# Decoder layer on one core: recurrence products moved from GpSimd to VectorE, two phases merged, and several smaller moves

## Chip, cores and metric

The kernel runs on one core of one Trainium2 chip. The time is that of one execution on the device in microseconds, from the runs of the same program. All times below that are placed inside an execution count from the first instruction of the profiled execution.

## What is computed

One layer of a decoder for 512 positions of width 1024, all in 32-bit floats. The part of the reference that matters here:

```python
h = rms_norm(x, g_pre_mix)
z = h @ w_in                                   # 512 x 1024 by 1024 x 9776 or so, cut in pieces
u, v, q, kv, nsa_g, xr, rg, mg = split(z)
y_a = gmlp_mixer(gelu(u), gelu(v), ...)        # LayerNorm of v, 128-position chunks, lower-triangular w_s
y_b = nsa_mixer(q, kv, nsa_g, ...)             # attention; its compress MLP: gelu((blocks + pe) @ w1) @ w2
y_c = rglru_mixer(xr, rg, ...)
merged = sum_k sigmoid(mg_k) * (y_k @ w_br_k)
x = x + rms_norm(merged @ w_o, g_post_mix)
f_gate, f_up = split(rms_norm(x, g_pre_ffn) @ w_ffn_in)
x = x + rms_norm((silu(f_gate) * f_up) @ w_ffn_out, g_post_ffn)

def rglru_mixer(xr, gate, ...):
    xc = conv4(xr) + conv_b                    # causal, per channel, along the positions
    r = sigmoid(xc @ w_a + b_a)                # 16 diagonal blocks of 64 x 64
    i = sigmoid(xc @ w_x + b_x)
    a = exp(-8 * r * softplus(-lam))
    b = sqrt(1 - a * a) * (i * xc)
    h[t] = a[t] * h[t - 1] + b[t]              # linear scan along the positions
    return h * gelu(gate)
```

## The kernel before

**Products.** Each product of 32-bit matrices is made of three TensorE products of rounded halves: high by high, high by low, low by high. `split` (L112 on) makes the halves: ScalarE copies the rounded high half (L114), VectorE subtracts it from the source for the low half (L119). The weights pass in tiles of 128x1024 (512 KB) through the sync engine's queue: `unit()` hands out the next weight tile, and `wload` fetches and splits two more ahead of it, with two buffers for the raw tile and three each for its halves. A tile of output is 24 products of 512 columns (8 blocks of the inner dimension by 3).

**Order.** The work is written as Python generators that `yield` at places where other work may be put between. `run(main, side, rate)` walks through the main generators and steps the side one `rate` times per yield. A main generator that yields a number n goes on a list: it has done its product, and its remaining steps come after n more yields of the main generators behind it, so that what it needs next from other engines can be made meanwhile. `seq` makes one side generator of several. The phases around the change are the calls of `run` from L1202 on:

```python
run([v_half(0), v_half(1), cmp_tile(0)], seq(norm(), load_wab()))
run(rnn(0, 0, 4), softplus())
run([gate_tile(), cmp_tile(1), cmp_tile(2)], seq(rec_batch(0), rec_out(0)))
run(rnn(1, 0, 4))
run([cmp_tile(3), gate_part("c", 0), compress(0), gate_part("c", 1)], seq(rec_batch(1), rec_out(1)))
```

**The recurrent branch.** It is cut in two halves of four tiles of 128 channels. `xr_tile` (L410) makes a tile's input product, the convolution on VectorE (L422), the split of the convolved rows (`ch` on ScalarE, `cl` on VectorE), and after `yield 3` the two gate products on TensorE (L430; bank `tr`, output R and TI). `rg_tile` makes the other input product and its gelu (GG). `rec_batch` (L439) then does the recurrence of a half: tanh, root and exponentials on ScalarE, and for each tile of 128x512 a small product on VectorE (L454), one on GpSimd (L455) and the scan on VectorE (L457). `rec_out` (L466) multiplies with the gelu on GpSimd (L473) and splits the result (`ych`, `ycl`) for the branch products.

**Beside it.** `gate_tile` makes the gates of the attention branches (`gsig`, transposed at L601), `cmp_tile` a part of the rows for compress (`xcmp`, copied by ScalarE at L623 and VectorE at L624), `compress` the small MLP of the attention: its first weights come as two 1 MB loads issued on ScalarE's queue (L630, tile `w`), its inputs are made by GpSimd's additions, its products are at L648, its hidden layer (`chid`) from L655 on. `gmlp_prep` (L480) loads the gMLP's triangle and bias (tile `gw`). `down` and its `close` (L1125) end the kernel: the last product, its sum of squares, the root, and the residual sum, by tiles of 128 positions in two halves of 512 columns.

**Buffers and banks.** SBUF tiles stand in pools by tag (slab 3, y 4, m 2, wab 2 buffers of 128x2048), PSUM in banks `mm` (6) and `tr` (2). Inside an engine the instructions run in the order in which they are issued, and across engines they are held by semaphores that the framework sets; the DMA issues of SP, ScalarE and GpSimd stand in those engines' own order.

## Time and profile before

| | |
|---|---|
| runs | 1162.02, 1164.91, 1165.14 us; median 1164.91 |
| profiled execution | 1168.17 us, of which the span of the instructions is 1166.4 us |
| mean granted TensorE clock in it | 0.991 of full speed |
| busy share | TensorE 98%, VectorE 59%, ScalarE 46%, GpSimd 5% |
| chain that ended last | TensorE 87% of the span, VectorE 7%, DMA 3%, ScalarE 2% |

The profiled execution is 3.3 us over the median of the runs. The rows below are of this one execution. In them PE is TensorE, PEld its weight loads, DVE VectorE, ACT ScalarE, POOL GpSimd, SP the sync engine; a name with q behind it (ACTq) is that engine's queue, where DMAs are issued. L12 is line 12 of the kernel before. Tiles bear the program's names.

### The profile page before, as it was taken

The page shows a single profiled execution, that of the slowest core. Times are in us where ns is not written, and L with a number is a line of the kernel's source. Part 1 is how long each engine was busy: PE and PEld are TensorE (multiplying, and loading weights), DVE is VectorE, ACT ScalarE, POOL GpSimd, SP SyncE. Part 2 cuts the span into 40 slices and gives each one's busy share as a digit, 9 for nine tenths or more (in the row PEclk, how much of TensorE's full clock was granted, in tenths as well). Part 3 has the DMA queues.
Part 4 walks back from the last instruction along what each step waited for, and adds up shares of the span by engine and source line. Part 5 has one row for each costly group of instructions (what it writes and reads, how often), then busy time and mean ns, then how long its engine had stood idle before and what let it go on. Part 6 is the DMA issues. An engine that isn't in the chain of part 4 may idle for free.

```text
span 1166.4 us, 14306 instructions
## 1 busy us (share of the span) xinstructions
PE 1140.9 (98%) x5524; PEld 949.6 (81%) x5524; DVE 690.6 (59%) x1266; ACT 532.8 (46%) x936; POOL 55.2 (5%) x55
## 2 busy tenths in 40 slices
PE   9999799999999999999999999999999999999997
PEld 7877578788888887888888788889988888888885
DVE  5974855545476799998898743557333323322324
ACT  6746446222244576877776523344323223232222
POOL 0000702510000000000000000000000000000001
PEclk9999989899999999999999999999999999999999
DMA  8332222522222211112111343332132232232231
GB/s 286 116 108 73 69 76 65 209 92 90 94 87 91 72 55 37 55 41 69 37 55 55 110 145 107 116 119 73 55 103 96 91 106 93 92 125 91 93 106 72
DMA packets 30373, 108.62 MB, mean 93 GB/s; under 512 B 3649, under 2 KB 3793, under 8 KB 29153
## 3 DMA queue, kind: packets, MB, share of 16 engines
q1 hardware_dynamic: 27792, 98.58, 25.7%
q10 hardware_dynamic: 2448, 9.05, 2.1%
q8 instruction: 43, 0.70, 0.2%
q14 instruction: 26, 0.20, 0.1%
q0 software_dynamic: 64, 0.08, 0.0%
HBM read 105.60 MB, written 2.10 MB: 92 GB/s over the span
## 4 chain that ended last, share of the span: by engine, by line
PE 87%; DVE 7%; DMA 3%; ACT 2%; issue 1%; POOL 1%; SPq 0%; DVEq 0%; ACTq 0%; POOLq 0%
PE mm L212 57%; PE mm L1122 10%; PE mm L1022 4%; PE sc L816 3%; PE o L854 3%; PE tr L841 3%; PE mm L732 2%; DVE lo L119 1%; PE tr L648 1%; PE tr L430 1%; DMA wabr<-in_wab 1%; DMA xrow<-in_x 1%; DVE ti L457 1%; PE tr L564 1%; DMA xt<-in_xT 1%
## 5 line engine op out<-in xcount | busy, mean ns | idle before, releaser
L114 ACT ACTIVATE hi<-raw 128x1024 fp32r<-128x1024 f32 (+1 forms) x162 | 170.8, 1054 | 357.6 <-PE mm L212 160.7
L119 DVE TENSOR_TENSOR lo<-raw,hi 128x1024 fp32r<-128x1024 f32 (+1 forms) x162 | 199.6, 1233 | 220.4 <-ACT hi L114 212.6
L212 PE MATMUL mm<-hh,lo 128*128 128x512 f32 x504 | 199.5, 396 | 2.5 <-DVE lo L119 2.5
L212 PE MATMUL mm<-hh,hi 128*128 128x512 f32 x504 | 200.5, 398 | 0.0
L212 PE MATMUL mm<-hl,hi 128*128 128x512 f32 x504 | 198.8, 395 | 0.0
L212 PE MATMUL mm<-fh,hi 128*128 128x512 f32 (+1 forms) x336 | 127.6, 380 | 0.0
L212 PE MATMUL mm<-fh,lo 128*128 128x512 f32 (+1 forms) x336 | 127.3, 379 | 0.0
L212 PE MATMUL mm<-fl,hi 128*128 128x512 f32 (+1 forms) x336 | 127.3, 379 | 0.0
L212 PEld LDWEIGHTS mm<-hh,lo 128*128 128x128 f32 x504 | 95.7, 190 | 22.8 <-DVE lo L119 3.4
L212 PEld LDWEIGHTS mm<-hl,hi 128*128 128x128 f32 x504 | 95.5, 189 | 18.9 <-issue 0.2
L212 PEld LDWEIGHTS mm<-hh,hi 128*128 128x128 f32 x504 | 95.6, 190 | 18.8 <-issue 0.2
L1122 PE MATMUL mm<-hi,f 128*128 128x512 f32 x320 | 99.4, 389 | 0.0
L822 ACT ACTIVATE P<-P,ast 128x128 f32<-128x128 f32 (+3 forms) x128 | 70.7, 555 | 23.2 <-DVE ast L820 22.6
L212 PEld LDWEIGHTS mm<-fh,lo 128*128 128x128 f32 x336 | 63.2, 188 | 12.0
L212 PEld LDWEIGHTS mm<-fh,hi 128*128 128x128 f32 x336 | 63.2, 188 | 11.8
L212 PEld LDWEIGHTS mm<-fl,hi 128*128 128x128 f32 x336 | 63.2, 188 | 11.7
L1122 PEld LDWEIGHTS mm<-hi,f 128*128 128x128 f32 x320 | 60.1, 188 | 12.4
L820 DVE CUSTOM_DVE_ANT_0 P<-sc,mask 128x128 f32<-128x128 f32 (+3 forms) x128 | 58.0, 485 | 8.2 <-PE sc L816 7.3
L1122 PE MATMUL mm<-lo,f 128*128 128x512 f32 x160 | 62.2, 389 | 0.0
L114 ACT ACTIVATE ph<-tr 128x512 fp32r<-128x512 f32 x80 | 47.0, 592 | 26.2 <-PE tr L841 25.2
L1079 DVE TENSOR_TENSOR silu<-silu,mm 128x512 f32<-128x512 f32 x22 | 15.1, 688 | 73.1 <-PE mm L212 73.1
L119 DVE TENSOR_TENSOR pl<-tr,ph 128x512 fp32r<-128x512 f32 x80 | 54.4, 686 | 2.8 <-ACT ph L114 1.0
(295 smaller groups left out, 1941.8 us busy)
## 6 DMA issues: line engine op xcount, KB each, us to landing
raw<-in_w_in SPq DMA_DIRECT2D x64, 512.0 KB, 3.5
raw<-in_w_fi SPq DMA_DIRECT2D x44, 512.0 KB, 3.5
raw<-in_w_br SPq DMA_DIRECT2D x24, 512.0 KB, 3.5
raw<-in_w_fo SPq DMA_DIRECT2D x22, 512.0 KB, 3.5
w<-in_cw ACTq DMA_DIRECT2D x4, 1024.0 KB, 6.6
raw<-in_w_o SPq DMA_DIRECT2D x8, 512.0 KB, 3.6
raw<-in_w_v SPq DMA_DIRECT2D x7, 512.0 KB, 5.6
xt<-in_xT SPq DMA_DIRECT2D x8, 256.0 KB, 7.4
```

What stands on the lines that cost most here:

```text
L114: SC.activation(hi, src, AF.Copy)
L119: res["lo"] = V.tensor_sub(lo, src, f32(hi))
L212: res["mm"] = PE.matmul(ps[:m, n0:n1], w[:, k * 128:k * 128 + m], x[k][:, n0:n1], start=(t == 0), stop=(t == 3 * NK - 1))
L732: PE.matmul(ps, x[k][:, q], w[:, ws], start=(k == 0 and t == 0), stop=(k == NK - 1 and t == 2))
L816: PE.matmul(ps[:, :w * n].rearrange("p (b n) -> p b n", b=w), lhs, K[:, i, brs[0]:brs[-1] + 1, :n], start=(i == 0), stop=(i == 1))
L820: V.tensor_tensor_reduce(out=t, in0=ps[:, b * n:b * n + n], in1=mask[0][:, S - n:], scale=-0.125, scalar=3.0e38, op0=OP.add, op1=OP.min, a ...
L822: SC.activation(t, t, AF.Exp, scale=-1.0, bias=st[:, 0, j, b:b + 1], accum_out=st[:, 1, j, b:b + 1])
L841: PE.transpose(pt[:, j * 128:(j + 1) * 128], self.part(j, br)[:, kt * 128:(kt + 1) * 128], ident)
L854: PE.matmul(po, VV[:, kt, g % 2, br].rearrange("p i d -> p (i d)"), x, start=(br == 0 and kt == 0 and t == 0), stop=(br == 1 and kt == a a ...
L1022: res["mm"] = PE.matmul(b[c, f], x[k][:, q], w[:, fs], start=(k == 0 and t == 0), stop=(k == NK - 1 and t == 2))
L1079: V.tensor_mul(s, s, pu)
L1122: PE.matmul(b[c], x[k][:, q], w[:, ws], start=(k == 0 and t == 0), stop=(k == NFF - 1 and t == 2))
```

## The change

Part by part:

- **Recurrence.** The product before each scan (`t * ti`) and the product with the gelu go from GpSimd to VectorE. The results of the two halves get slabs of their own (`yc["h", b]`, `yc["l", b]`) instead of two pairs that both halves share; the R slab of the second half takes a buffer of tag `y` instead of `m`.
- **Merging.** The third and the fourth `run` become one, with the side work at a rate of 0.45 steps per yield.
- **Gates.** `yield 3` ahead of the gate products becomes `yield 4`.
- **Small loads.** The second weights and position vectors of compress get tiles of their own and are fetched on GpSimd's queue in both calls; the gMLP's triangle and bias move from the sync engine's queue to GpSimd's. The bank of the gMLP's column sums is one of `mm` instead of `tr`.
- **Start.** The first half of the first weight tile is fetched on ScalarE's queue and the vector of constants on the sync engine's; the load of the first weights is issued before the constants are made; 11 warm-up products instead of 9.
- **End.** `close` forms the product with the gain on VectorE straight from PSUM for both column halves, takes the root on ScalarE with the sum of the first half as bias, and makes one step of Newton with the gain scaled by -0.5. The last tile's first column half is stored in two pieces.

```diff
-                SY.dma_start(raw[:, p], ap[:, p])
+                (SC if i == n == 0 else SY).dma_start(raw[:, p], ap[:, p])
...
-    SC.dma_start(vec, A["vec"])
+    SY.dma_start(vec, A["vec"])
+    wload(1)
...
-    for _ in range(9):
+    for _ in range(11):
         PE.matmul(pw[:, :128], ones, ones, start=True, stop=True)
...
-            rec[b] = dict(R=slab("r", tag="m"), GG=slab("gg", tag="m"), TI=slab("ti"))
+            rec[b] = dict(R=slab("r", tag="y" if b else "m"), GG=slab("gg", tag="m"), TI=slab("ti"))
...
-        yield 3
+        yield 4
...
-            GP.tensor_mul(t, t, ti)
+            V.tensor_mul(t, t, ti)
...
-        if b == 0:
-            yc["h"], yc["l"] = Pair("ych", F32R, "y"), Pair("ycl", F32R, "y")
+
+        yc["h", b], yc["l", b] = slab("ych", F32R, "y"), slab("ycl", F32R, "y")
...
-            GP.tensor_mul(y, rec[b]["TI"][:, c, :], rec[b]["GG"][:, c, :])
-            split(y, yc["h"][4 * b + c], yc["l"][4 * b + c])
+            V.tensor_mul(y, rec[b]["TI"][:, c, :], rec[b]["GG"][:, c, :])
+            split(y, yc["h", b][:, c, :], yc["l", b][:, c, :])
...
-        SY.dma_start(wsT, A["wsT"])
-        SY.dma_start(rwb[:, 1], A["bs"])
+        GP.dma_start(wsT, A["wsT"])
+        GP.dma_start(rwb[:, 1], A["bs"])
...
-        ps = bank("tr")
+        ps = bank("mm")
...
-        w2 = mid.tile([128, 2, 64], F32, tag="cw2", name=nm("cw2"), bufs=1)
-        (GP if kv == 0 else SC).dma_start(w2, A["cw2"][kv])
-        pe = mid.tile([128, 1, 32], F32, tag="cpe", name=nm("cpe"), bufs=1)
-        (GP if kv == 0 else SC).dma_start(pe[:, 0], A["cpe"][kv])
+        w2 = const0([128, 2, 64], nm("cw2"))
+        GP.dma_start(w2, A["cw2"][kv])
+        pe = const0([128, 1, 32], nm("cpe"))
+        GP.dma_start(pe[:, 0], A["cpe"][kv])
...
+                V.tensor_scalar(res["gf"][i], res["gf"][i], -0.5, None, op0=OP.mult)
...
-            SC.activation(j, b[c], AF.Square, accum_out=res["ss"][:, f, c:c + 1])
+            SC.activation(j, b[c], AF.Square, accum_out=ss[:, f, c:c + 1])
+            V.tensor_mul(y, b[c], res["gf"][f])
             if f == 0:
-                V.tensor_mul(y, b[c], res["gf"][f])
-            else:
-                ss = res["ss"]
-                V.tensor_add(ss[:, 0, c:c + 1], ss[:, 0, c:c + 1], ss[:, 1, c:c + 1])
-                i = rsqrt(ss[:, 2, c:c + 1], ss[:, 0, c:c + 1], 1, 1.0 / D, EPS, root=True)
-                with tc.issue_after(i.ins):
-                    SC.activation(y, b[c], AF.Copy)
-                GP.tensor_mul(y, y, res["gf"][f])
...
+                V.tensor_scalar(ss[:, 3, c:c + 1], ss[:, 0, c:c + 1], 1.0 / D, EPS, op0=OP.mult, op1=OP.add)
+                return
...
+            SC.activation(root, ss[:, 1, c:c + 1], AF.Sqrt, scale=1.0 / D, bias=ss[:, 3, c:c + 1])
+            V.tensor_scalar(a, ss[:, 1, c:c + 1], 1.0 / D, ss[:, 3, c:c + 1], op0=OP.mult, op1=OP.add)
+            V.reciprocal(r, root)
+
+            V.scalar_tensor_tensor(u, r, a, r, op0=OP.mult, op1=OP.mult)
+            V.scalar_tensor_tensor(r, u, -3.0, r, op0=OP.add, op1=OP.mult)
+            cut = [(1, 0, 512), (0, 0, 512)] if c < 3 else [(1, 0, 512), (0, 0, 256), (0, 256, 512)]
...
-    run([gate_tile(), cmp_tile(1), cmp_tile(2)], seq(rec_batch(0), rec_out(0)))
-    run(rnn(1, 0, 4))
+    run([gate_tile(), cmp_tile(1), cmp_tile(2)] + rnn(1, 0, 4), seq(rec_batch(0), rec_out(0)), 0.45)
     run([cmp_tile(3), gate_part("c", 0), compress(0), gate_part("c", 1)], seq(rec_batch(1), rec_out(1)))
+    yc["h"], yc["l"] = ([yc[n, k // 4][:, k % 4, :] for k in range(NK)] for n in "hl")
```

What this does to the order of the instructions shows at three places. Names carry a buffer's number, and the lines of the changed kernel are up to 8 lower than those of before.

The first is VectorE between the recurrence of the first half and the first convolution of the second (`xc` the convolved rows, `cl` their low half, `lo` the low half of a weight tile, `ycl` that of the branch's rows). Before:

```order
L119 TENSOR_TENSOR ycl_1081<-yc_165_1097,ych_1079 128x512
L119 TENSOR_TENSOR ycl_1081<-yc_166_1107,ych_1079 128x512
L624 COPY xcmp_559<-mm_1066 64x32x8
L119 TENSOR_TENSOR lo_1128<-raw_1125,hi_1127 128x1024
L624 COPY xcmp_559<-mm_1066 64x32x8
L119 TENSOR_TENSOR lo_1168<-raw_1165,hi_1167 128x1024
L422 SCALAR_TENSOR_TENSOR xc_1155<-mm_1124,vec,xc_1155 128x511
L422 SCALAR_TENSOR_TENSOR xc_1155<-mm_1124,vec,xc_1155 128x510
L422 SCALAR_TENSOR_TENSOR xc_1155<-mm_1124,vec,xc_1155 128x509
L119 TENSOR_TENSOR cl_1161<-xc_1155,ch_1160 128x512
```

Now (the scan is the row that ends in `ti_599<-r_597,t_1002`):

```order
L449 SCALAR_TENSOR_TENSOR ti_599<-r_597,t_1002 128x512
L616 COPY xcmp_559<-mm_1059 64x32x8
L446 SCALAR_TENSOR_TENSOR t_1002<-r_597,t_1002 128x512
L119 TENSOR_TENSOR lo_1104<-raw_1101,hi_1103 128x1024
L447 TENSOR_TENSOR t_1002<-t_1002,ti_599 128x512
L119 TENSOR_TENSOR lo_1147<-raw_1144,hi_1146 128x1024
L414 SCALAR_TENSOR_TENSOR xc_1134<-mm_1100,vec,xc_1134 128x511
L449 SCALAR_TENSOR_TENSOR ti_599<-r_597,t_1002 128x512
L414 SCALAR_TENSOR_TENSOR xc_1134<-mm_1100,vec,xc_1134 128x510
L414 SCALAR_TENSOR_TENSOR xc_1134<-mm_1100,vec,xc_1134 128x509
L119 TENSOR_TENSOR lo_1190<-raw_1187,hi_1189 128x1024
L119 TENSOR_TENSOR cl_1140<-xc_1134,ch_1139 128x512
```

The splits of the branch's rows (two of the four show here) and the products with the gelu have gone behind the convolution, and two scans with their products stand in and ahead of it.

The second is TensorE at the first gate product of the second half (`tr` its bank, `mm` the input product that stands around it). Before:

```order
L212 MATMUL mm_1164<-hh_120,lo_1070 128x512
L212 MATMUL mm_1164<-hh_120,hi_1069 128x512
L212 MATMUL mm_1164<-hl_122,hi_1069 128x512
L430 MATMUL tr_1189<-ch_1160,wabh_495 128x512
L212 MATMUL mm_1164<-hh_120,lo_1070 128x512
L212 MATMUL mm_1205<-hh_119,hi_1127 128x512
L430 MATMUL tr_1189<-cl_1161,wabh_495 128x512
L430 MATMUL tr_1189<-ch_1160,wabl_496 128x512
```

Now:

```order
L212 MATMUL mm_1186<-hh_126,lo_1104 128x512
L212 MATMUL mm_1186<-hh_126,hi_1103 128x512
L422 MATMUL tr_1199<-ch_1139,wabh_495 128x512
L212 MATMUL mm_1186<-hl_128,hi_1103 128x512
L212 MATMUL mm_1186<-hh_126,lo_1104 128x512
L212 MATMUL mm_1186<-hh_126,hi_1103 128x512
L212 MATMUL mm_1186<-hl_128,hi_1103 128x512
L212 MATMUL mm_1186<-hh_126,lo_1104 128x512
L422 MATMUL tr_1199<-cl_1140,wabh_495 128x512
L422 MATMUL tr_1199<-ch_1139,wabl_496 128x512
```

The gate products now come inside the input product of a later weight tile instead of at the change from one to the next, and five products of the input stand between the first and the other two instead of two.

The third is ScalarE at the first weights of compress (`xcmp` the copies of the rows, `hi` the high half of a weight tile, `tg` a tanh for the branch gates). Before:

```order
L449 ACTIVATE r_1121<-r_1121,spm_183 128x512 x4
L623 ACTIVATE xcmp_559<-mm_1472 64x32x8
L114 ACTIVATE hi_1525<-raw_1523 128x1024
L623 ACTIVATE xcmp_559<-mm_1472 64x32x8
L630 DMA w_236_1561<-in_cw 128x2048
L972 ACTIVATE tg_1559<-mm_1522 128x512
L630 DMA w_237_1562<-in_cw 128x2048
```

Now:

```order
L441 ACTIVATE r_1097<-r_1097,spm_183 128x512 x4
L615 ACTIVATE xcmp_559<-mm_1470 64x32x8
L114 ACTIVATE hi_1523<-raw_1521 128x1024
L622 DMA w_234_1559<-in_cw 128x2048
L615 ACTIVATE xcmp_559<-mm_1470 64x32x8
L964 ACTIVATE tg_1557<-mm_1520 128x512
L622 DMA w_235_1560<-in_cw 128x2048
```

The first of the two loads stands ahead of the second copy instead of behind it; the second keeps its place behind the tanh.

## Rows read from the trace of the kernel before

**Rows 1.** the page's first part: busy us (share of span) xinstructions:

```profile
PE 1140.9 (98%) x5524; PEld 949.6 (81%) x5524; DVE 690.6 (59%) x1266; ACT 532.8 (46%) x936; POOL 55.2 (5%) x55
```

**Rows 2.** waits of TensorE: engine line waited for: us, times, longest:

```profile
PE tr L430 <- ACT ch L114: 6.5, 2, 5.5
PE tr L648 <- DMA w<-in_cw: 2.9, 1, 2.9
PE mm L212 <- DVE lo L119: 2.5, 2, 1.9
...
PE tr L601 <- ACT gsig L597: 0.8, 1, 0.8
```

**Rows 3.** windows: stretch, us, busy PE PEld DVE ACT POOL, PEclk, DMA, GB/s:

```profile
134.66:138.07 3.41, 3.41 (x10) 2.67 (x9) 3.38 (x5) 1.58 (x2) 3.33 (x4) 0.50 0.50 154
144.90:151.73 6.83, 5.52 (x13) 4.41 (x14) 3.05 (x4) 2.87 (x4) 0.00 (x0) 0.50 0.39 137
206.34:213.17 6.83, 6.07 (x22) 5.57 (x23) 4.42 (x5) 1.26 (x2) 4.20 (x4) 0.50 0.50 210
```

**Rows 4.** chain of waits: start us, us, what (a stretch at full clock):

```profile
663.02 87.08 PE mm L212 x384
```

**Rows 5.** timeline of VectorE: start, us, operation [idle before <-releaser]:

```profile
119.14 2.31 DVE L457 TENSOR_TENSOR_SCAN ti<-r,t 128x512 f32<-128x512 f32 x1 [1.19 <-POOL t L455]
...
131.68 1.23 DVE L457 TENSOR_TENSOR_SCAN ti<-r,t 128x512 f32<-128x512 f32 x1 [1.19 <-POOL t L455]
132.82 1.20 DVE L119 TENSOR_TENSOR lo<-raw,hi 128x1024 fp32r<-128x1024 f32 x1
...
134.73 4.07 DVE L119 TENSOR_TENSOR ycl<-yc,ych 128x512 fp32r<-128x512 f32 x4
138.83 0.63 DVE L624 COPY xcmp<-mm 64x256 f32<-64x256 f32 x1
...
143.12 2.32 DVE L422 SCALAR_TENSOR_TENSOR xc<-mm,vec,xc 128x511 f32<-128x511 f32 x3
146.19 0.69 DVE L119 TENSOR_TENSOR cl<-xc,ch 128x512 fp32r<-128x512 f32 x1 [0.76 <-ACT ch L114]
```

**Rows 6.** timeline of TensorE, first product of the gate tile:

```profile
109.18 0.40 PE L591 MATMUL mm<-hh,hi 128*128 128x512 f32 x1
```

**Rows 7.** timeline of ScalarE, recurrence of the first half:

```profile
111.37 1.28 ACT L445 ACT_TABLE_LOAD   x1
...
118.97 1.05 ACT L114 ACTIVATE hi<-raw 128x1024 fp32r<-128x1024 f32 x1
```

**Rows 8.** compress weights: ScalarE's timeline, then the tile view of w:

```profile
201.72 0.82 ACTq L630 DMA_DIRECT2D w<-in_cw  x2
...
DMA to landing us min/median/max: 5.2/6.6/8.2
```

**Rows 9.** timeline of VectorE; DMA issues (KB each, median us to landing):

```profile
242.59 0.86 DVE L487 TENSOR_SCALAR gw<-gw 128x512 f32<-128x512 f32 x1
244.12 0.41 DVE L656 SCALAR_TENSOR_TENSOR chid<-chid,tr 128x248 f32<-128x248 f32 x1 [0.67 <-ACT chid L655]
...
gw<-in_bs SPq DMA_DIRECT2D x1, 256.0 KB, 3.0
cw<-in_cw POOLq DMA_DIRECT2D x1, 64.0 KB, 4.8
...
vec<-in_vec ACTq DMA_DIRECT2D x1, 56.0 KB, 3.7
cpe<-in_cpe POOLq DMA_DIRECT2D x1, 16.0 KB, 6.7
```

**Rows 10.** the end: timelines of ScalarE, then VectorE:

```profile
1158.71 0.60 ACT L1128 ACTIVATE junk<-mm 128x512 f32<-128x512 f32 x1 [3.75 <-PE mm L1122]
...
1160.54 1.22 DVE L276 SCALAR_TENSOR_TENSOR ss<-rs_t,ss 128x1 f32<-128x1 f32 x1
1161.80 1.42 DVE L1141 SCALAR_TENSOR_TENSOR yo<-yo,ss,xr 128x512 f32<-128x512 f32 x2
```

More of the change, by code (lines that the diff above doesn't have):

```diff
@@ L256, in hybrid_block, with rsqrt @@
                      channel_multiplier=1)
-    epsb = const.tile([128, 1], F32, name="epsb")
-    V.memset(epsb, EPS)
-    def rsqrt(dst, src, n, scale, eps, root=False):
+    def rsqrt(dst, src, n, scale, eps):
         a = const.tile([128, 8], F32, tag="rs_a", name=nm("rs_a"), bufs=2)[:, :n]
@@ L266, in rsqrt @@
         V.tensor_scalar(a, src, scale, eps, op0=OP.mult, op1=OP.add)
-        if root:
-            first = SC.activation(t, src, AF.Sqrt, scale=scale, bias=epsb)
-            V.reciprocal(dst, t)
-        else:
-            V.tensor_scalar(ib, a.bitcast(I32), 1, None, op0=OP.logical_shift_right)
-            V.tensor_scalar(dst.bitcast(I32), ib, -1.0, float(0x5F3759DF), op0=OP.mult, op1=OP.add)
-        for _ in range(1 if root else 3):
+        V.tensor_scalar(ib, a.bitcast(I32), 1, None, op0=OP.logical_shift_right)
+        V.tensor_scalar(dst.bitcast(I32), ib, -1.0, float(0x5F3759DF), op0=OP.mult, op1=OP.add)
+        for _ in range(3):
             V.tensor_mul(t, dst, dst)
@@ L276, in rsqrt @@
             V.scalar_tensor_tensor(dst, t, 1.5, dst, op0=OP.add, op1=OP.mult)
-        return first if root else None
     def spread(ps, col):
@@ L298, in scaled @@
         V.scalar_tensor_tensor(gl[k], xt[k], g, f32(gh[k]), op0=OP.mult, op1=OP.subtract)
-    wload(1)
     x_in(3)
@@ L1125, in close @@
         def close(c):
+            ss = res["ss"]
             y = res["y"].t[f][:, c, :]
             j = row("junk")
[L1128 removed]
+            SC.activation(j, b[c], AF.Square, accum_out=ss[:, f, c:c + 1])
+            V.tensor_mul(y, b[c], res["gf"][f])
             if f == 0:
[L1130 to L1142 removed]
+                V.tensor_scalar(ss[:, 3, c:c + 1], ss[:, 0, c:c + 1], 1.0 / D, EPS, op0=OP.mult, op1=OP.add)
+                return
+            t = const.tile([128, 3], F32, tag="cl", name=nm("cl"), bufs=2)
+            root, a, u = (t[:, i:i + 1] for i in range(3))
+            r = ss[:, 2, c:c + 1]
+            SC.activation(root, ss[:, 1, c:c + 1], AF.Sqrt, scale=1.0 / D, bias=ss[:, 3, c:c + 1])
[4 more added lines that the diff above has]
+            cut = [(1, 0, 512), (0, 0, 512)] if c < 3 else [(1, 0, 512), (0, 0, 256), (0, 256, 512)]
+            for n, (i, lo, hi) in enumerate(cut):
+                y = res["y"].t[i][:, c, lo:hi]
+                fs = slice(i * 512 + lo, i * 512 + hi)
+                V.scalar_tensor_tensor(y, y, r, res["x"][c][:, fs], op0=OP.mult, op1=OP.add)
+                (SC if n == 1 else SY).dma_start(out[c * 128:(c + 1) * 128, fs], y)
         for i in range(n - last):
```

6 lines of the change are left out of this document (removed).

## The prediction

> **What bounds the kernel now.** I began with the page's busy shares: TensorE is busy for 98% of the span [rows 1], so nothing but its idle time, its time at a low clock and the two ends can be won. The second view is who TensorE waited for [rows 2]: 6.5 us for the high half of the convolved rows (two waits, 5.5 and 1.0), 2.9 us for the compress weights, 2.5 us for the low halves of two weight tiles (the longer 1.9), 0.8 us for the branch gates. The reader sees four names for 12.7 us, all of them before 210 us. The third view is the granted clock [rows 3]: in three stretches it is 0.50, the 1.2 GHz level. The first begins 0.6 us after the wait of 1.9 us has ended, the others inside the waits of 5.5 and 2.9 us. Busy time in them is 3.41, 5.52 and 6.07 us; at 2.4 GHz it would take half, so they cost 1.7, 2.8 and 3.0 us. The wait of 1.0 us was followed by no such stretch. Elsewhere a matmul of 512 columns takes 87.08 / 384 = 0.227 us [rows 4], and there the change cannot help. The most that it can win is thus the 12.7 us of waits, 7.5 us of low clock, and something at the end.
>
> **The change, part by part.**
>
> Recurrence on VectorE. Sixteen products of 128x512 leave GpSimd for VectorE at 0.69 us each, the price of a subtraction with two SBUF inputs [rows 5]: 11 us more work there. Against it stands what GpSimd's products cost VectorE. The same scan took 2.31 us while GpSimd multiplied and 1.23 us when GpSimd was still, and four subtractions took 4.07 us beside GpSimd's additions, 1.02 instead of 0.69 each [rows 5]. I take 1.23 for the scans.
>
> Merging. The order on VectorE decides when the first tile of the second half gets its gates. I replay it by hand from the gate tile on, which TensorE begins at 109.2 [rows 6]; I allow 0.2 more. ScalarE before: root table 1.28 at 111.37, ..., weights of the next tile done at 118.97 + 1.05 = 120.0 [rows 7]. The new order puts the gate's sigmoid among the exponentials: two table loads (2.6) and one 512-column activation (0.6, as the square of [rows 10]) more ahead of those weights, so 123.2. TensorE gets there after 16 + 48 matmuls and the small transposes, at 109.4 + 14.5 + 0.4 = 124.3: in time. The second tile's weights follow on ScalarE 1.6 us later, about 0.3 us late. VectorE starts on the low half at about 123.7 and then has, up to the last convolution step: four low halves (4 x 1.20), four copies (4 x 0.63), three scans (3 x 1.23), two small products (2 x 0.69) and three steps (2.32) [rows 5], together 14.7, so 138.4; ScalarE's high half (0.6) makes 139.0. TensorE reaches the gate product after 24 + 24 + 7 matmuls, 124.6 + 12.5 = 137.1, and waits 1.9 us. The next need, the low half, costs 1.20 + 0.69 more on VectorE, 140.9, against TensorE's 139.0 + 6 x 0.227 = 140.4: 0.5 at most, half of it taken. Sum of waits 0.3 + 1.9 + 0.2 = 2.4. A wait as long was followed by a stretch of 3.41 us at 1.2 GHz [rows 3], so I charge 1.7. Before, this place cost 0.8 + 2.5 + 5.5 in waits and 1.7 + 2.8 in clock, 13.3; now 4.1. **Gain 9.2**, between 5.3 (VectorE 2.2 us later than my sum, two slow stretches) and 13.3.
>
> What else hangs on these steps: GpSimd's sixteen additions for compress stay where they are, but begin only after the last scan has freed their buffer, at about 137, so they meet the low halves behind it (1.0 instead of 0.69), not the scans. The products with the gelu and their splits now stand behind the first gate product. They are needed only by the branch products some 75 us later, which is their cover. In the second half the last low half for the branch product comes at about 216.5 by the same prices, just when TensorE asks for it: the tightest place that is left.
>
> Compress weights. Before, both issues stood at 201.72 on ScalarE's queue, behind a copy that waits for VectorE [rows 8]; 5.2 us to landing is 206.9, where TensorE's wait of 2.9 us ended. Now the first stands right behind the weights at about 198.5: 203.7 by the quickest landing, 205.1 by the median of 6.6. TensorE arrives at 206.9 - 2.9 = 204.0. The second half is needed some 3.8 us later and lands at 201 + 6.6 = 207.6. **Gain 5.9**: 2.9 of wait and 3.0 of clock; the lower bound is 3.0, if 1 us of wait and one stretch stay.
>
> Gates a part later. In the first half the product comes seven matmuls (1.6 us) later, so its high half is there; but its three products now stand together, and the second needs the low half, 0.69 us [rows 5] behind. **Gain 0.3** of 1.0, between 0 and 1.0.
>
> Small vectors by GpSimd's queue. The compress vectors are fetched at the start and need nothing after that. The two loads for the gMLP leave the sync engine's queue, where the weights behind them no longer wait; no TensorE wait stood on those, so this is worth nothing. On their landing hangs VectorE's scaling at 242.59, and behind it the hidden layer of compress with 0.67 us of slack [rows 9]. On GpSimd's queue 64 KB took 4.8 us and 16 KB 6.7, on ScalarE's at the same crowded time 56 KB took 3.7 [rows 9]. So the landing is 1.1 to 3.0 us later, and the loss 0.4 to 2.3; I take **0.5 lost**, since the larger transfer is the nearer one. By the Trainium skill (DMA: Bandwidth & Descriptors, Anatomy of one DMA) such a transfer takes 2.0 us plus its bytes at 436 GB/s; for 256 KB that is an estimate of 2.6 us, below the 3.0 us of the row for the sync engine's queue, so by the page nothing is lost here and the sum would be 0.5 us better. The two rows of GpSimd's queue lie far above that, and I keep them.
>
> The end. Before, 1161.80 + 1.42 - 1158.71 = 4.5 us went from the last square to the last output product; in it a product of one element took 1.22 us beside GpSimd's multiplication [rows 10]. Now: square 0.7 with its read, product with the gain 0.7, four small steps of 0.2, one output product 0.75 and two halves 0.8, together 3.75. **Gain 0.8**, between 0.5 and 1.3 (the last store is half as long). The gain's two scalings wait on VectorE for a load whose cover is the wait for TensorE's last up product.
>
> The start. A load is moved ahead on another queue, but the same bytes stand before the first weights that TensorE needs. Two more warm-up products fill idle time. The bank changed from one pool to another has no wait in the trace. All three: nothing, within 0.5 both ways.
>
> **Sum.** 9.2 + 5.9 + 0.3 - 0.5 + 0.8 = 15.7 us. The profiled execution's span of 1166.4 becomes 1150.7, its time of 1168.17 becomes 1152.5. The median shown is 1164.91, 3.3 us below that execution; from it the forecast is **1149.2**.
>
> **Rivals.**
> 1. All waits go: VectorE is 2 us quicker than my sum, or idle time that short does not slow the clock. Gain 13.3 + 5.9 + 1.0 + 1.3 = 21.5: **1143.4**. For it: the replay misses by only 1.9 us, and the prices are of single rows. Against: I left out what passes between instructions.
> 2. VectorE is later and the gate product waits over 4 us, with two slow stretches, and half of the compress gain stays out: 5.3 + 3.0 - 2.3 + 0.5 = 6.5: **1158.4**. For it: VectorE is busy without a gap for 20 us there.
> 3. Slower than before: the scan is slow by itself, not by GpSimd. At 2.31 each and with 0.69 more per product, VectorE is behind by 4 x (1.08 + 0.69) = 7.1 us in each half beyond the replay's prices. The first gate product then waits 9.0 instead of 1.9 and the last low half of the branch product 7.1, each with 5 us more of low clock than I charge: 15.7 - 24.2 = -8.5, **1173**. It decides from about 4 us of extra delay in each half. Against: one scan at 1.23 stands in the trace with GpSimd idle.
> 4. GpSimd's queue is starved: the loads for the gMLP land 3.0 us later or more, the clock drops, and 2.3 + 1.7 instead of 0.5 is lost: **1152.7**. The Trainium skill (SBUF — State Buffer, SBUF: two separate sides) says that GpSimd cannot write descriptors while VectorE runs an operation in a mode of two ports, and gives 3.1 us in place of 0.62 for a load that met such an operation. Against: VectorE waits for just this load and runs nothing then.
> 5. The change does not do what it says: the order on the chip puts the weights' issue and the first gate back behind the same work, and gains and losses cancel: within 3.5 us of **1164.9**.
>
> **How the numbers follow.** No change can be told from one within about 0.3%, 3.5 us. Forecast 48%, rival 1 20%, rival 2 16%, rival 4 8%, rival 5 5%, rival 3 3%. Faster: 48 + 20 + 16 + 8 = 92%; same 5%; slower 3%. The range runs from rival 1 to rival 2, 1143.4 to 1158.4, with rival 4 inside; outside are rivals 3 and 5 and the tails.
>
> **What would show it.** Scans at 1.23 us throughout; one wait of about 2 us for the high half of the convolved rows near 137 and at most one slow stretch behind it; none for the compress weights and no slow stretch near 207; half a microsecond for the hidden layer of compress near 230; 3.8 us from the last square to the last output product. I am wrong if scans stay above 2 us, if there is a slow stretch at the compress weights, or if a new name leads TensorE's waits.

## The result, and the profile after

The changed kernel takes **1148.28 us** (median of 4 runs, 1148.07 to 1148.75), the kernel before in the same set 1163.98 (1162.02 to 1165.14). The ratio is 0.9867, with a 95% interval of 0.985 to 0.9884. The forecast was 1149.2 in a range of 1143.4 to 1158.4.

The profiled execution took 1148.33 us with a span of 1146.6, against 1168.17 and 1166.4 before. So the two traces differ by 19.8 us and the medians by 15.7: the traced execution of before was a long one, and a second trace of it (first experiment) has a span of 1161.3. The forecast's sum, 15.7, meets the medians. Against the trace from which it was worked out, several of its terms were too small, one was too large, and 1.1 us at the head stood in none of them. Where the gain lies shows when the span is cut at products that every kernel issues in the same order: the last product of the head (the 64th of `hi` by `gxh`), the 16th, 65th, 116th and 186th of `hh` by `hi` (the 65th opens the gate tile, as [rows 6]), the first score of the attention, TensorE's last end and the end of the span.

| us from cut to cut | before | before, second trace | after |
|---|---|---|---|
| head, to the last product of w_v's first part | 51.7 | 50.6 | 50.6 |
| on to the 16th | 16.3 | 16.3 | 16.3 |
| gates of the first half, to the gate tile | 41.2 | 40.8 | 39.3 |
| recurrence of the first half and change to the second | 48.8 | 47.8 | 37.2 |
| second half, compress weights, branch rows | 83.0 | 80.0 | 78.6 |
| branch products, gMLP, change to attention | 151.6 | 151.6 | 151.6 |
| all that follows on TensorE | 766.1 | 766.4 | 766.2 |
| behind TensorE's last product | 7.8 | 7.8 | 6.6 |

The work of each engine (the page's first part) has hardly changed; only GpSimd's has gone from 55.2 to 24.0 us, and VectorE's is the same with eighteen instructions more, the sixteen products among them [rows 1]:

```profile
PE 1133.5 (99%) x5528; PEld 945.5 (82%) x5528; DVE 689.8 (60%) x1284; ACT 533.3 (47%) x934; POOL 24.0 (2%) x39
```

What TensorE waited for has (columns as in [rows 2]):

```profile
PE tr L422 <- ACT ch L114: 1.7, 1, 1.7
PE mm L212 <- DVE ycl L119: 1.3, 1, 1.3
```

Of the four names of before one is left, for the high half of the convolved rows, and a new one has come: the last low half of the branch's rows.

Windows around the first wait, and around the compress weights and the second wait (columns as in [rows 3]), show a granted clock of 1.00 throughout:

```profile
134.20:138.00 3.80, 2.15 (x10) 1.64 (x10) 3.77 (x6) 2.23 (x4) 0.00 (x0) 1.00 0.38 126
189.00:206.00 17.00, 15.71 (x101) 13.64 (x100) 15.95 (x18) 5.58 (x9) 9.20 (x8) 1.00 0.42 162
```

The three stretches at 0.50 [rows 3] have no counterpart here, nor is there one anywhere else between the head's first product and the last.

On VectorE the recurrence of the first half now reads like this, and behind it ScalarE's high half of the convolved rows (columns as in [rows 5]):

```profile
130.09 0.68 DVE L447 TENSOR_TENSOR t<-t,ti 128x512 f32<-128x512 f32 x1
...
132.61 1.22 DVE L449 TENSOR_TENSOR_SCAN ti<-r,t 128x512 f32<-128x512 f32 x1
```

```profile
135.34 0.63 ACT L114 ACTIVATE ch<-xc 128x512 fp32r<-128x512 f32 x1 [0.42 <-DVE xc L414]
```

The scan takes 1.22 us, like the one of before that ran while GpSimd was idle (1.23), and the product ahead of it 0.68. The high half is there at 135.34 + 0.63 = 135.97; TensorE had stood since 134.37 and went on at 136.02.

Some 60 us later GpSimd adds the position vectors for the second call of compress, and VectorE's operations are long again:

```profile
195.22 3.16 DVE L119 TENSOR_TENSOR ycl<-yc,ych 128x512 fp32r<-128x512 f32 x3
...
199.34 3.20 DVE L119 TENSOR_TENSOR lo<-raw,hi 128x1024 fp32r<-128x1024 f32 x2
202.46 1.10 DVE L119 TENSOR_TENSOR ycl<-yc,ych 128x512 fp32r<-128x512 f32 x1
```

Three low halves of rows take 1.05 us each instead of 0.63 to 0.69, two low halves of weight tiles 1.60 instead of 1.22; the last row is the one that TensorE waits for. On ScalarE the first load of the compress weights now stands among the exponentials, and the second still behind the second copy:

```profile
180.26 0.72 ACT L441 ACTIVATE r<-r,spm 128x512 f32<-128x512 f32 x1
180.28 0.34 ACTq L622 DMA_DIRECT2D w<-in_cw  x1
180.89 1.94 ACT L441 ACTIVATE r<-r,spm 128x512 f32<-128x512 f32 x3
...
185.35 0.66 ACT L615 ACTIVATE xcmp<-mm 64x256 f32<-64x256 f32 x1 [1.13 <-DVE xcmp L616]
185.36 0.33 ACTq L622 DMA_DIRECT2D w<-in_cw  x1
```

The loads for the gMLP took 3.0 us from issue to landing on GpSimd's queue, like the slower of them before, and VectorE waited 0.33 us for them; the hidden layer's 0.67 us of idle time is unchanged [rows 9]:

```profile
gw<-in_wsT POOLq DMA_DIRECT2D x1, 256.0 KB, 3.0
gw<-in_bs POOLq DMA_DIRECT2D x1, 256.0 KB, 3.0
cw<-in_cw POOLq DMA_DIRECT2D x2, 64.0 KB, 5.9
...
cpe<-in_cpe POOLq DMA_DIRECT2D x2, 16.0 KB, 6.1
```

```profile
224.10 0.44 DVE L479 TENSOR_SCALAR gw<-gw 128x512 f32<-128x512 f32 x1 [0.33 <-DMA gw<-in_bs]
225.21 0.41 DVE L648 SCALAR_TENSOR_TENSOR chid<-chid,tr 128x248 f32<-128x248 f32 x1 [0.67 <-ACT chid L647]
```

The end, from the last square to the last output product, is 1142.07 + 1.54 - 1139.98 = 3.6 us against 4.5 [rows 10]:

```profile
1139.98 0.60 ACT L1124 ACTIVATE junk<-mm 128x512 f32<-128x512 f32 x1 [4.42 <-PE mm L1116]
```

```profile
1141.87 0.16 DVE L1137 SCALAR_TENSOR_TENSOR ss<-cl,ss 128x1 f32<-128x1 f32 x1
1142.07 1.54 DVE L1142 SCALAR_TENSOR_TENSOR yo<-yo,ss,xr 128x512 f32<-128x512 f32 x3
```

### The profile page after: what moved, and what is told of

The parts are those of the page before. It is cut to its first block, busy times and chain, and to the rows that moved or that the text cites. A ratio compares the mean times of both kernels' runs of the same rounds, so it can differ in the third digit from the quotient of the medians.

```text
span 1146.6 us, 14314 instructions
## 1 busy us (share of the span) xinstructions
PE 1133.5 (99%) x5528; PEld 945.5 (82%) x5528; DVE 689.8 (60%) x1284; ACT 533.3 (47%) x934; POOL 24.0 (2%) x39
## 4 chain that ended last, share of the span: by engine, by line
PE 90%; DVE 6%; ACT 3%; DMA 1%; issue 1%; SPq 0%; DVEq 0%; ACTq 0%
PE mm L212 59%; PE mm L1116 10%; PE mm L496 3%; PE sc L808 3%; PE o L846 3%; PE tr L833 3%; PE mm L724 2%; PE mm L1014 2%; DVE lo L119 1%; PE tr L422 1%; DVE ti L449 1%; DMA raw<-in_w_v 1%; PE tr L556 1%; PE tr L640 1%; PE tr L746 1%
```

## The experiments

The theory after the result: the products on VectorE free the scans from GpSimd and carry most of the gain, at the phase change and at the compress weights. The main rival was that merging does it. The small parts were then undone one by one. Where kernels are compared by stretches, the cuts are those of the table above; a table at the end of this section gives them all. A set is the runs that were taken together; a median is best compared with one of its own set.

**A second trace of the kernel before** (no edit).

> The kernel before, unchanged, for a second profile of it. Theory: the profiled execution that the prediction read was a long one (1168.17 us against runs of 1162.02 to 1165.14), because the stretches at 1.2 GHz differ from one execution to the next; a second profile shows the same four waits (5.5, 2.9, 1.9 and 0.8 us, each within 0.3), a span of 1160.5 to 1164 and at least one stretch at 0.50 less than three. Rival: the stretches are tied to the waits and the long execution had longer waits; then the second profile shows three stretches again and waits that are shorter by 2 us or more in sum.

One run, 1163.02 us, span 1161.3. Its waits, and windows at the wait of 1.88 us, in and behind the long wait, and at the compress weights:

```profile
PE tr L430 <- ACT ch L114: 7.8, 2, 7.0
PE tr L648 <- DMA w<-in_cw: 2.7, 1, 2.7
PE mm L212 <- DVE lo L119: 2.5, 2, 1.9
```

```profile
130.78:132.66 1.88, 0.00 (x2) 0.00 (x1) 1.85 (x3) 0.00 (x0) 1.09 (x1) 1.00 0.00 0
141.23:148.06 6.83, 3.28 (x8) 2.60 (x9) 5.19 (x7) 2.86 (x4) 0.91 (x1) 0.50 0.37 133
201.76:206.00 4.24, 1.54 (x14) 1.57 (x15) 3.99 (x3) 0.63 (x1) 3.02 (x3) 1.00 1.01 422
```

The theory held, but for the longest wait, which is 7.0 us instead of 5.5: there is one stretch at 0.50 instead of three. Waits of 1.9 and 2.7 us stand here without a stretch, where nearly the same waits, 1.9 and 2.9, had one in the first trace. So what a wait costs in clock differs from one execution of this kernel to the next, and a sum that is read from one trace takes over that execution's share.

**The products back on GpSimd**, phases merged:

```diff
-            V.tensor_mul(t, t, ti)
+            GP.tensor_mul(t, t, ti)
...
-            V.tensor_mul(y, rec[b]["TI"][:, c, :], rec[b]["GG"][:, c, :])
+            GP.tensor_mul(y, rec[b]["TI"][:, c, :], rec[b]["GG"][:, c, :])
```

> The changed kernel with its sixteen products of the recurrence and of the gelu back on GpSimd, all else as changed (merged phases too). Theory (the products carry the gain at the compress weights and part of that at the phase change): scans are back at up to 2.3 us, the first weights of compress are issued behind the second copy again and TensorE waits 2 to 3 us for them with a stretch at 1.2 GHz behind it (5.7 us lost together), and the first gate product of the second half waits 3 to 8 us more than the 1.65 us it does now: 1157 to 1162 us. Rival (merging alone did it): within 1.5 us of 1148.3.

1159.43 us (5 runs, 1158.51 to 1161.23), as the theory said, but not all for its reasons. TensorE's waits:

```profile
PE mm L212 <- DVE u L382: 3.3, 1, 3.3
PE tr L640 <- DMA w<-in_cw: 2.8, 1, 2.8
PE mm L212 <- DVE lo L119: 2.1, 1, 2.1
PE tr L422 <- ACT ch L114: 1.4, 1, 1.4
```

The compress weights are late again: both loads are issued at 190.43 us, behind a copy that waited 2.89 us for VectorE, and that stretch is 3.4 us longer than after.

```profile
190.43 0.65 ACT L615 ACTIVATE xcmp<-mm 64x256 f32<-64x256 f32 x1 [2.89 <-DVE xcmp L616]
190.43 0.82 ACTq L622 DMA_DIRECT2D w<-in_cw  x2
```

But the wait for the convolved rows is no longer than after (1.4 us), with scans of 2.31 and 2.12 us. Merging had made up for them. The wait of 2.1 us for a low half stands beside it, so the phase change costs 2.6 us more in all. The first line of the waits was in no expectation: 3.3 us for a gelu product of the gMLP, at the change to the attention. More on it below.

**The phases apart**, products on VectorE:

```diff
-    run([gate_tile(), cmp_tile(1), cmp_tile(2)] + rnn(1, 0, 4), seq(rec_batch(0), rec_out(0)), 0.45)
+    run([gate_tile(), cmp_tile(1), cmp_tile(2)], seq(rec_batch(0), rec_out(0)))
+    run(rnn(1, 0, 4))
```

> The changed kernel with the two phases apart again (side work at rate 1 in the first, none in the second), products on VectorE. Theory: VectorE has four products with the gelu and four splits, 0.6 us each, ahead of the first convolution step again, so the first gate product waits 4 to 7 us instead of 1.65, with one stretch at 1.2 GHz behind it (up to 3 us); the gates' sigmoid costs TensorE 0.8 us again; the compress weights stay early, without a wait. 1153 to 1157 us. Rival (the products alone did it): within 1 us of 1148.3.

1149.69 us (4 runs, 1148.69 to 1150.74), ratio to before 0.9881 (0.9863 to 0.9899), which overlaps the changed kernel's. The theory fell here: merging is worth about 1.3 us by the stretch at the phase change (38.6 against 37.2), not 5 to 9. The waits:

```profile
PE tr L422 <- ACT ch L114: 1.8, 1, 1.8
PE mm L212 <- DVE ycl L119: 1.3, 1, 1.3
PE mm L212 <- DVE lo L119: 1.3, 1, 1.3
```

The wait for the convolved rows is 1.8 us, not 4 to 7. Four products and four splits are ahead of the convolution again, but VectorE is fast enough for them, with scans at 1.2 us; what comes back is a wait of 1.3 us for a low half of a weight tile.

**Less work for VectorE, first try:**

```diff
-                V.tensor_copy(dst[64:128], src[:, :, :, 1])
+                SC.activation(dst[64:128], src[:, :, :, 1], AF.Copy)
...
-            SC.dma_start(w1[i], A["cw1"][kv, :, 8 * i:8 * i + 8, :])
+            (GP if kv == 0 else SC).dma_start(w1[i], A["cw1"][kv, :, 8 * i:8 * i + 8, :])
```

> The changed kernel with two more edits: VectorE's copies of the compress rows go to ScalarE (twelve of 64x256, 0.63 us each) and the two loads of the first compress weights go from ScalarE's queue to GpSimd's, so that they do not stand behind those copies. Theory (both waits that are left, 1.65 us at the first gate product and 1.28 us at the last low half of the branch's rows, are VectorE's load): both vanish, 1145 to 1146.5 us. Rival 1 (ScalarE is the later one then): a new wait for a high half of a weight tile of 1 to 2 us, 1147 to 1148.5. Rival 2 (1 MB loads on GpSimd's queue land late): the wait for the compress weights is back, 1150 or more.

1154.04 us (4 runs, 1151.65 to 1156.17), a miss. Both waits that were left did vanish, and the phase change is 1.9 us shorter. But two others came:

```profile
PE mm L212 <- DVE u L382: 3.3, 1, 3.3
PE tr L655 <- DVE chid L650: 2.8, 1, 2.8
```

The compress weights land early, so TensorE comes to the second layer of compress (L655) sooner, and its hidden layer waits on VectorE behind the rows' low halves; and the 3.3 us at the change to the attention are there again. With each of the two stands a stretch at 1.2 GHz, of 6.83 and 3.41 us. Neither of the rivals had named these.

**The other bank undone:**

```diff
-        ps = bank("mm")
+        ps = bank("tr")
         PE.matmul(ps, ones, wsT.rearrange("p g t -> p (g t)"), start=True, stop=True)
```

> The changed kernel with the bank of the gMLP's column sums back in tr, nothing else. Theory (learnt from the two runs in which a wait of 3.3 us stood at the phase change, on VectorE's last gelu product of the gMLP): which banks the last tiles of one phase leave is set by the count of mm banks before, and with tr the first tile of the next phase gets the bank that is freed last. A wait of 3.3 us near 340, with a stretch at 1.2 GHz behind it or without (1.7 to 3.4 us): 1151.5 to 1155 us. Rival (the step of the prediction: the bank is worth nothing): within 0.5 us of 1148.3.

1153.55 us (4 runs, 1152.43 to 1154.45), 5.3 over the changed kernel, whose runs are of another set. TensorE's wait, VectorE's product that ends it, and the clock behind it:

```profile
PE mm L212 <- DVE u L382: 3.3, 1, 3.3
```

```profile
340.12 0.69 DVE L382 SCALAR_TENSOR_TENSOR u<-gs,mm 128x512 f32<-128x512 f32 x1 [0.70 <-ACT gs L381]
```

```profile
342.11:345.52 3.41, 3.41 (x9) 2.63 (x8) 0.78 (x2) 0.63 (x1) 0.00 (x0) 0.50 0.00 0
```

The last u product of the gMLP ends at 337.6; the first product of the next phase starts at 340.86, when VectorE has read that tile's bank for the last time (340.12 + 0.69). 3.26 us of waiting and half of 3.41 make 5.0, and the stretch is 5.1 longer (156.7 against 151.6). So this line of the change, which the prediction held for nothing, is worth 5 us in the changed kernel. Over all the traces the wait stands where the products are on VectorE and the bank is in `tr` (two kernels) or the products on GpSimd and the bank in `mm` (one), and not where they are on GpSimd and `tr` (two) or on VectorE and `mm` (seven); the one exception is the first try above, in which other copies moved too. Why an operation's engine changes which bank is the last to come free is left open; it was not tried.

**The products alone**, in the kernel before:

```diff
-            GP.tensor_mul(t, t, ti)
+            V.tensor_mul(t, t, ti)
...
-            GP.tensor_mul(y, rec[b]["TI"][:, c, :], rec[b]["GG"][:, c, :])
+            V.tensor_mul(y, rec[b]["TI"][:, c, :], rec[b]["GG"][:, c, :])
```

> The kernel before with one part of the change alone: its sixteen products of the recurrence and of the gelu on VectorE. Theory: the products are what wins at the phase change of the recurrence and at the compress weights (as the changed kernel without merging already shows): no wait for the compress weights, the first gate product waits 2 to 4 us instead of 5.5 to 7.0, scans at 1.2 us; but without the other bank a wait of 3.3 us comes up near 345 and gives a third of it back. 1153 to 1158 us. Rival (merging and the small parts carry the gain): 1161 us or more.

1158.62 us (4 runs, 1157.05 to 1158.92), 6.0 under the 1164.64 of before in the same set. Its waits, and the scans and loads that explain them:

```profile
PE mm L212 <- DVE u L390: 3.3, 1, 3.3
PE tr L430 <- ACT ch L114: 2.4, 2, 1.7
PE mm L212 <- DVE ycl L119: 1.3, 1, 1.3
```

```profile
119.78 1.21 DVE L457 TENSOR_TENSOR_SCAN ti<-r,t 128x512 f32<-128x512 f32 x1
```

```profile
184.62 0.33 ACTq L630 DMA_DIRECT2D w<-in_cw  x1
```

The time is 0.6 us above the theory's range. In the traced execution, 1158.92 us, the clock rose only after 10.7 us and the head is 1.6 us longer than that of the changed kernel; whether the other three runs share that is not shown. The mechanism is as the theory said: scans at 1.21 us with nothing else changed, no wait for the compress weights (first load issued at 184.62, among the exponentials), and 3.3 us given back at the change to the attention, with 1.7 of clock behind it. The wait for the convolved rows is 1.7 us there, less than the 2 to 4 expected, and one of 1.3 us for a low half of a weight tile stands beside it. By stretches the phase change gains 9 to 10 us (38.6 against 47.8 and 48.8).

**Merging alone**, in the kernel before (the merged line of the change for the two).

> The kernel before with one part of the change alone: the two phases merged at rate 0.45, products still on GpSimd. Theory (merging and moving the products are two ways to the same thing at the phase change, only the products help at the compress weights): the first gate product waits 1 to 2.5 us instead of 5.5 to 7.0, a low half of a weight tile about 2 us, the compress weights still 2.7 us; no wait at the change to attention, since the banks fall as before. 1156.5 to 1160 us. Rival (merging gains only with the products on VectorE): 1161 us or more.

1156.15 us (4 runs, 1155.24 to 1156.74), 8.2 under the 1164.36 of before in the same set, a little below what was expected. The waits:

```profile
PE tr L430 <- ACT ch L114: 3.3, 3, 2.4
PE tr L648 <- POOL yc L473: 2.4, 1, 2.4
PE mm L212 <- DVE lo L119: 2.1, 1, 2.1
```

The phase change takes 40.5 us, 7 to 8 less than before, with scans still slow; the compress weights wait as before. (The second line names GpSimd's product, which ended at 196.97; both loads were issued at 192.15 us and took 4.8 at the least, and TensorE, which here reads the loads and not that product, went on at 197.11.) Merging and moving the products are thus two cures for the same ill at the phase change: each alone takes 7 to 10 us, both together 10 to 12.

**The gates a part earlier** (`yield 4` back to `yield 3`).

> The changed kernel with the gate products a part earlier again (yield 3). Theory of the prediction: 0.3 us slower, 1148.6. Rival (from the offsets of the two traces: between 57 and 106 us the changed kernel gains 1.8 us, of which one wait explains 1.06): 1.5 to 2 us slower or more, 1149.8 to 1151 us, with waits for the high half of the convolved rows at the first tile of the first half and more than one in the second half.

1151.77 us (4 runs, 1149.71 to 1152.73), 3.5 over the changed kernel, whose runs are of another set. In the trace the stretch of the first half is 4.7 us longer than after, 44.0 against 39.3: a wait of 2.4 us for the first convolved rows, 1.7 us for a stretch of 3.41 us at 1.2 GHz behind it, and 0.6 over the other three tiles.

```profile
PE tr L422 <- ACT ch L114: 4.3, 3, 2.4
```

The step of the prediction falls; the rival was right in direction and still too small. In the four traces with `yield 3` and the old start the same wait was 0.6 to 1.1 us; why it is longer here is left open.

**The old end:** `close`, the root and the unscaled gain as before.

> The changed kernel with the end of before (close, the root with one step of Newton, the gain unscaled, last tile in two halves). The prediction's step: 0.8 us slower, 1149.1, between 0.5 and 1.3. The offsets of the two traces say 1.1 us. Rival (the stores' own landing hides it): no difference, 1148.3 within 0.3.

1150.29 us (4 runs, 1149.17 to 1151.22). Behind TensorE's last product 7.6 us stand instead of 6.6, 1.0 more. The median is 2.0 us above the changed kernel's, but that was of another set: in this one the two kernels that differ least from it (the gMLP's loads and the old start, below) took 1149.66 and 1148.82. The product of one element beside GpSimd's multiplication is back:

```profile
1141.95 1.22 DVE L277 SCALAR_TENSOR_TENSOR ss<-rs_t,ss 128x1 f32<-128x1 f32 x1
```

**The old start**, and **the gMLP's loads on the sync engine's queue**.

> The changed kernel with the start of before (first half of the first weight tile on the sync engine's queue, the constants' vector on ScalarE's, the load of the first weights behind the constants, 9 warm-up products). The prediction's step: nothing, within 0.5 us of 1148.3. Rival (the offsets of the two traces): 0.6 to 1.1 us slower, by a wait of about 0.8 us at the third weight tile, 1148.9 to 1149.4; and if TensorE's clock rises later after the shorter warm-up, up to 2 us more.

1148.82 us (4 runs, 1148.12 to 1149.91). The head takes 50.6 us, as after; over all traces it is 50.5 to 52.2 with the old start (5 of them) and 49.9 to 51.5 with the new (9). No difference can be told from that scatter, and no effect of the longer warm-up on when the clock rises: 4.7 to 5.0 us after the start with 9 products, and once 10.7; 4.0 to 7.0 with 11. The new start moves a wait: in the five traces with the old one TensorE waits 0.9 to 1.6 us for the high half of the first weight tile, in the nine with the new one never; but in five of these it waits 0.5 to 1.1 us for that of the second tile, and with the old start in one of five, 0.8.

> The changed kernel with the two loads of the gMLP back on the sync engine's queue. The prediction's step: 0.5 us faster (between 0.4 and 2.3), 1146 to 1147.9. Rival (the load lands in time on either queue, as VectorE's wait of 0.33 us for it in the changed kernel and the unchanged 0.67 us ahead of the hidden layer say): no difference, 1148.3 within 0.4.

1149.66 us (4 runs, 1148.61 to 1150.39), and a span of 1146.6, that of the changed kernel. The queue makes no difference, as the rival said.

**Less work for VectorE, second try:** only the first half's copies move, the weights stay on ScalarE's queue, and the additions for the second call of compress go to ScalarE, into a tile with a buffer of tag `m`.

```diff
-                V.tensor_copy(dst[64:128], src[:, :, :, 1])
+                if i < 3:
+                    SC.activation(dst[64:128], src[:, :, :, 1], AF.Copy)
+                else:
+                    V.tensor_copy(dst[64:128], src[:, :, :, 1])
...
-        X = [slab("x1", shape=(G, 8, 32)), comp[kv]]
+        X = [slab("x1", tag="m" if kv else "slab", shape=(G, 8, 32)), comp[kv]]
...
-            for g in range(G):
+            for r in range(8 * kv):
+                SC.activation(X[i][:, :, r, :], comp[kv][:, :, r, :], AF.Identity, bias=pe[:, 0, 16 * i + 2 * r:16 * i + 2 * r + 1])
+            for g in range(0 if kv else G):
```

> The changed kernel with two edits: VectorE's eight copies of the compress rows in the first half go to ScalarE, and GpSimd's eight additions for the second call of compress go to ScalarE as sixteen with a bias per partition. Theory: the two waits that are left (1.65 us for the high half of the convolved rows, 1.28 us for the last low half of the branch's rows) are VectorE's load, in the second place as lengthened by GpSimd's additions beside it (low halves of rows 1.05 us instead of 0.68, of weights 1.58 instead of 1.22); both vanish, no wait at the phase change, 1145 to 1146.2 us. Rival 1 (ScalarE becomes the late one): a wait of 1 us or more for a high half or for compress's inputs, 1146.5 to 1149. Rival 2 (the slower operations came from elsewhere): the second wait stays, 1146.6.

**1145.28 us** (5 runs, 1144.22 to 1146.11), ratio to before 0.9836 (0.9823 to 0.985), the fastest of all. No wait of over 0.3 us is left between the head and the attention, and the second stretch of VectorE shows why:

```profile
193.85 1.89 DVE L119 TENSOR_TENSOR ycl<-yc,ych 128x512 fp32r<-128x512 f32 x3
...
196.26 2.36 DVE L119 TENSOR_TENSOR lo<-raw,hi 128x1024 fp32r<-128x1024 f32 x2
198.53 0.69 DVE L119 TENSOR_TENSOR ycl<-yc,ych 128x512 fp32r<-128x512 f32 x1
```

With GpSimd idle, three low halves of rows take 0.63 us each instead of 1.05, and two of weights 1.18 instead of 1.60: GpSimd's additions had made them long. The Trainium skill (SBUF — State Buffer, SBUF: two separate sides) says that VectorE and GpSimd share a pair of ports under an exclusive lock, which a VectorE operation with two SBUF inputs takes against a GpSimd operation that reads SBUF. The rows agree that such operations of VectorE take longer beside GpSimd. In one the whole operation of GpSimd shows: in the kernel before, the product of one element [rows 10] and GpSimd's multiplication beside it end together, at 1161.76 and 1161.74 us, and the product took 1.22 us instead of the 0.16 of its neighbours.

```profile
1160.48 1.26 POOL L1137 TENSOR_TENSOR yo<-yo,gf 128x512 f32<-128x512 f32 x1 [4.14 <-ACT yo L1136]
```

Scans and subtractions took a third to nine tenths longer than alone.

Not undone alone were the slabs of their own and the compress vectors' new queue. The table bears on both: before + products and after, phases apart, differ in them, among other things, and take 38.6 us each at the phase change, 78.6 and 78.3 at compress.

All kernels by stretches, in us (columns in the order of the first table, without the 16.3). The medians are of four sets, in which the kernel before took 1163.98, 1163.06, 1164.64 and 1164.36:

| kernel | head | gates | phase change | compress | to attention | rest | end | median |
|---|---|---|---|---|---|---|---|---|
| before | 51.7 | 41.2 | 48.8 | 83.0 | 151.6 | 766.1 | 7.8 | 1163.98 |
| before, second trace | 50.6 | 40.8 | 47.8 | 80.0 | 151.6 | 766.4 | 7.8 | 1163.02 |
| before + products | 52.2 | 40.7 | 38.6 | 78.6 | 156.7 | 766.0 | 7.7 | 1158.62 |
| before + merging | 50.5 | 40.7 | 40.5 | 80.2 | 151.6 | 766.4 | 7.7 | 1156.15 |
| after | 50.6 | 39.3 | 37.2 | 78.6 | 151.6 | 766.2 | 6.6 | 1148.28 |
| after, products on GpSimd | 50.1 | 40.2 | 39.8 | 82.0 | 158.1 | 766.2 | 6.7 | 1159.43 |
| after, phases apart | 50.2 | 39.7 | 38.6 | 78.3 | 151.6 | 766.1 | 6.7 | 1149.69 |
| after, bank in tr | 51.1 | 39.4 | 37.3 | 78.6 | 156.7 | 766.3 | 6.6 | 1153.55 |
| after, yield 3 | 49.9 | 44.0 | 37.2 | 78.8 | 151.6 | 766.1 | 6.7 | 1151.77 |
| after, old end | 51.0 | 39.3 | 37.2 | 78.6 | 151.6 | 766.0 | 7.6 | 1150.29 |
| after, old start | 50.6 | 39.3 | 37.2 | 78.4 | 151.6 | 766.2 | 6.6 | 1148.82 |
| after, gMLP loads on sync | 50.6 | 39.3 | 37.3 | 78.6 | 151.6 | 765.9 | 7.0 | 1149.66 |
| first try | 51.5 | 39.3 | 35.3 | 82.4 | 156.7 | 765.8 | 6.8 | 1154.04 |
| second try | 51.4 | 39.9 | 35.3 | 76.5 | 151.7 | 766.3 | 6.9 | 1145.28 |

## Why the prediction was right, and where its steps were not

The time was right, and so were the direction and the places: by the stretches all but 1.1 us at the end and the scatter of the head was won between 68 and 241 us of the first trace, at waits and low clock. Step by step, in the prediction's words:

- **"I take 1.23 for the scans."** Right: 1.22 after, and 1.21 to 1.23 in the kernel before with the products alone moved. Rival 3 (the scan is slow by itself) is refuted by that run.
- **Merging and recurrence, "gain 9.2".** The replay by hand was close: counted from the start of the gate tile, the high half came after 29.7 us (135.97 - 106.23) where it had 29.6 (139.0 - 109.4), and the gate product waited 1.65 us instead of 1.9. The 1.7 us charged for low clock were not spent, and the other two small waits (0.3 and 0.2) did not come, so the stretch gained 11.6 against the first trace and 10.6 against the second. What the term did not say is that its two halves overlap: given the products, merging brings only 1.3 us.
- **Compress weights, "gain 5.9".** The mechanism was right: the first load moved ahead (180.28 us against a product at 189.3) and the wait went. But the stretch gained 4.4 us against the first trace and 1.4 against the second. The 3.0 us of low clock belong to one execution of before and not to the other, and 1.3 us were given back in the new wait for the last low half. The prediction had called that "the tightest place that is left" and charged nothing; its 216.5 by "the same prices" left out that GpSimd's additions for the second call of compress stand beside exactly these operations.
- **"begin only after the last scan has freed their buffer, at about 137, so they meet the low halves behind it (1.0 instead of 0.69)".** Off: GpSimd's additions for the first call of compress began at 150.51 us, released by VectorE's last product with the gelu of that half, and all four low halves of the branch's rows took 0.68 to 0.69. No term of the sum hung on it.
- **Gates a part later, "gain 0.3".** Mis-sized: 1.5 to 1.9 us against the two traces of before, and 3.5 by the medians when it is undone in the changed kernel. The high half was late in the first tile by 0.6 to 1.1 us in the four traces with `yield 3` and the old start, and three tiles lost 0.2 to 0.3 more each; the second product's need of the low half cost nothing.
- **Small vectors, "0.5 lost".** Nothing was lost. The load took 3.0 us on GpSimd's queue. The rows taken for it, 4.8 and 6.7 us, were of the crowded start, where the same queue took 5.9 and 6.1 us in the changed kernel too, and so of another neighbourhood. The page of the Trainium skill that was weighed there (DMA: Bandwidth & Descriptors, Anatomy of one DMA) leads to the estimate of 2.6 us, nearer to the measured 3.0 than the two rows. Rival 4 is refuted with it: VectorE waited 0.33 us.
- **"The bank changed from one pool to another has no wait in the trace. [...] nothing."** Wrong, and the largest error: undoing it costs 5.3 us. The trace of before has no such wait; moving the products alone brings it, 3.3 us and 1.7 of clock, and with this line it is gone. The forecast missed the price and its cure together, and so they cancelled.
- **The end, "gain 0.8"**: 1.0 to 1.1. **The start, "nothing"**: nothing that stands out of the scatter.

Rival 1 (all waits go) came true only with the second try, which lies 3.0 us under the changed kernel. Rivals 2 and 5 did not come: no wait over 1.7 us is left in the places that they name, and the first weights' issue did move.

That the sum of 15.7 equals the difference of the medians is in part luck. It was made on an execution with three stretches at 1.2 GHz, where 19.8 us were to be had; on the second trace there were 14.7. And against the first trace, terms that were too small (by 2.4 at the phase change, 1.6 at the gates, 0.5 for the load, 0.3 at the end) stand against one that was too large, by 1.5 at the compress weights.

## What to carry to other kernels

GpSimd's elementwise work is not free for VectorE: cost it by what it does to VectorE's operations beside it, here 1.2 to 2.3 us for a scan and 0.63 to 1.05 for a subtraction, and look where it lands before it is moved or left. When two edits attack the same wait, try each alone; here either took most of the gain. After any edit look at the change of phases too, since which PSUM bank a tile gets can move a wait of 3 us to a place that no edited line touches.

## What was not expected

- A wait for the bank that is freed last, 3.3 us at the change to the attention, came and went with edits to work that is done 100 us and more earlier, and cost 5.1 to 6.5 us with the clock: the same 3.26 us were followed by a stretch of 3.41 us at 1.2 GHz in three kernels and of 6.83 in one.
- The same wait was followed by a stretch at 1.2 GHz in one execution and not in another: 1.88 us with 3.41 in the first trace of before and none in the second; 2.9 with 6.83, and 2.7 with none. In the changed kernel, whose waits are 1.65 and 1.28 us, the trace shows none there, and its four runs lie within 0.7 us, those of before within 3.1.
